# Gate matrices read back eight first keys at a time into two buffers, and scores of 88 and 80 first keys kept in DRAM

## The chip, the cores and the metric

One Trainium2 chip, one of its cores. The metric is the device time of one execution in microseconds (us), as the median of several. The core has five engines with queues of their own: PE (matrix multiplies; PEld is its weight load), DVE, ACT and POOL (element-wise work), and SP, which only issues transfers. Each engine runs its instructions in a fixed order.

## What is computed

Two layers. In each a mixer (attention, a Fourier branch and a convolution branch) is followed by an expert retrieval, and the change lies in that retrieval. There are 128 x 128 experts; an expert's number is a first key times 128 plus a second key. Every token picks 16 experts in each of 8 heads and gets for each a gate; the result sums what the chosen experts give:

```python
s_top, i_top = lax.top_k(s, PEER_TOPK)
best, pos = lax.top_k(cand, PEER_TOPK)
eid = jnp.take_along_axis(cand_id, pos, axis=-1)
gate = jax.nn.softmax(best, axis=-1).astype(hc.dtype)
u = jnp.take(u_tab, eid, axis=0)
act = jax.nn.gelu(jnp.einsum('chkd,cd->chk', u, hc)) * gate
v = jnp.take(v_tab, eid, axis=0)
return jnp.einsum('chk,chkd->cd', act, v)
```

All of it is float32: tables of 16384 x 1024 for u and for v in each layer, 512 tokens in layer 0 and 256 in layer 1.

## The kernel before, in words

Layer 0 handles its first 128 tokens by fetching the chosen rows (`gather_u`, `gather_v`: 128 fetches from u_tab and 128 from v_tab by POOL, each followed by one DVE instruction). The other 384 tokens of layer 0 and all 256 of layer 1 go the dense way: every expert's score is computed, multiplied by a gate that is zero for the experts not chosen, and multiplied with v.

Dense work runs over the 128 first keys i. For each, `scores` loads a 512 KB tile of u (L218, queue SP), splits it into a high part (`whi`, ACT, L237) and a low part (`wlo`, POOL or DVE, L243), and runs 24 matrix multiplies `su` (8 chunks, 3 each, L257 to L259). ACT applies gelu.

First stretch, `dense_u`: for the first `count` keys (`SPILL`: 92 in layer 0, 84 in layer 1) the scores go to a buffer `sst` (L978) and from there to DRAM (`sd`). Beside it, by `weave` at L1161, runs the retrieval (`retrieve`, nearly all DVE) of each group of 128 tokens and `gates`, which builds the gate matrix: 32 steps for a group, each two DVE instructions (`oij` L941, `og` L944), 8 small multiplies `pw` (L954) and one ACT copy `wst` (L957); every 8 steps a 2 MB piece goes to DRAM (`wd`). In layer 0 also 78 steps of the row fetching are woven in. `weave` writes the keys, the retrieval steps and the fetch steps in proportion: of the 92 keys of layer 0, 4 come first, 80 are spread over 246 retrieval steps, 8 follow; of the 84 of layer 1, 4, 68 over 164 steps, and 12. A scheduler then fixes each engine's order, which keeps near to the written one; `behind` keeps the fetches and the `pw` from running ahead of the keys.

Second stretch, `dense_v`: it goes over all 128 keys, first the 36 (layer 0) or 44 (layer 1) whose scores are not in DRAM, which `values` computes on the spot (`snew`, L1007), then the others, whose scores are read back (`srd`, L1010, two keys each). The gate matrices come back with `wrd` (L1026): one load brings `WB` = 4 first keys, in runs of 4 x 32 numbers, 512 bytes, 768 KB in layer 0 and 512 KB in layer 1, into one of three buffers. Per key a 512 KB tile of v is loaded and split, DVE multiplies score and gate (`xa`, L1031), ACT and DVE split the product (`xh`, `xl`), and PE adds it with 18 (layer 0) or 12 (layer 1) multiplies `yacc` into accumulators that stay over all keys. `values` runs `AHEAD` = 2 keys before its use.

Loads of u and v go through a ring of `raw` buffers, 4 KB of each partition: in `dense_u` of layer 0 four of them, in its `dense_v` two more, six (L1170, `more_rings`); in `dense_v` of layer 1 eight. A load waits on SP until the buffer's last split is done, and all that stands behind it on SP waits with it. In layer 0's `dense_u` all `wlo` are made by POOL, in layer 1's every third by DVE.

Of the kernel before, what the change touches and what calls it, by code (L numbers as in the profile page):

```python
# [9 lines left out]
F32 = mybir.dt.float32  # L10
# [15 lines left out]
P = 128  # L26
# [8 lines left out]
NCAND = 50  # L35
GRID_W = 64
TG = 32
WB = 4
OH = 4


# [107 lines left out]
def body(ctx: ExitStack, tc, nc, a, out):  # L149
# [837 lines left out]
    def dense_v(l, pp, vs, early, cols, count, sd, wd):  # L987

        c0, c1 = cols
        n = c1 - c0  # L990
        ng = n // TG

        banks = (2, 3, 4, 5, 0, 1) if l < L - 1 else range(4)
        acc = {k: (mm if at < 4 else tp)("yacc") for at, k in enumerate(banks)}
        seq = list(range(count, NK)) + list(range(count))

        def scratch():
            return pp.tile([P, n], F32, name="n0_sq", tag="xa", bufs=3)

        got = {}  # L1000

        def values(i):
            if i >= count:
                p = sm("su")
                scores(l, i, cols, p, G)
                got[i] = vs.tile([P, n], F32, name="snew", bufs=AHEAD + 1)
                S.activation(out=got[i], in_=p[:, :n], func=AF.Gelu_apprx_tanh)  # L1007
            elif i % 2 == 0:
                s = vs.tile([P, 2, n], F32, name="srd", bufs=4)
                SP.dma_start(out=s, in_=sd[i // 2])  # L1010
                got[i], got[i + 1] = s[:, 0], s[:, 1]

        def products(k, i, v, xh, xl, first, last):
            t, g = k // 2, k % 2
            mm3(acc[k], (xh[:, t * P:(t + 1) * P], xl[:, t * P:(t + 1) * P]),
                (v[0][:, g * 512:(g + 1) * 512], v[1][:, g * 512:(g + 1) * 512]), first, last)

        for i in seq[:AHEAD]:
            values(i)
        late = []  # L1020
        for at, i in enumerate(seq):
            if at + AHEAD < NK:
                values(seq[at + AHEAD])
            if i % WB == 0:
                w = vs.tile([P, ng, WB, TG], F32, name="wrd", bufs=3)
                SP.dma_start(out=w, in_=wd[:, :, i:i + WB].rearrange("g j i t -> j g i t"))  # L1026
            v = split(raw(a["v_tab"][(l * NK + i) * NK:(l * NK + i + 1) * NK]), lo_eng=V if i % 2 or l < L - 1 else G)
            x = pp.tile([P, n], F32, name="xa", bufs=3)
            xh = pp.tile([P, n], F32R, name="xh", bufs=TAIL)
            xl = pp.tile([P, n], F32R, name="xl", bufs=TAIL)  # L1030
            V.tensor_tensor(out=x.rearrange("p (g t) -> p g t", t=TG), in0=got.pop(i).rearrange("p (g t) -> p g t", t=TG), in1=w[:, :, i % WB], op=ALU.mult)  # L1031
            pace["DVE"] = split_to(xh, xl, x)
            if at < NK - TAIL:
                for k in range(len(acc)):
                    products(k, i, v, xh, xl, at == 0, False)
            else:
                late.append((i, v, xh, xl))
            yield
        early.close()
        pending = []  # L1040
        for k in banks:
            for it in late:
                products(k, *it, False, it is late[-1])
            for f in pending:
                f()
            pending = []
            if l < L - 1 and k == 0:
                order["dve"] = rsqrt(pp, rsb, pm[:, :NS], NS, 1.0 / D, "n0", [scratch()[:, :NS] for _ in range(3)])
            y = pp.tile([P, 512], F32, name="yv", bufs=2)
            S.copy(out=y, in_=acc[k])  # L1050
            f0, t0 = k % 2 * 4, c0 + k // 2 * P
            residual(l, y, f0, t0)
            if l == L - 1:
                SP.dma_start(out=out[:, f0:f0 + 4, t0 - NS:t0 - NS + P], in_=xT[:, f0:f0 + 4, t0:t0 + P])
                continue
            if k == 4:
                pm = mm("n0_cs")
            if k in (4, 5):
                for c in range(f0, f0 + 4):
                    pending.append(col_square(scratch()[:, :NS], pm[:, :NS], xT[:, c, NS:], c == 0, c == 7))  # L1060
# [27 lines left out]
            yield from g  # L1088


    SPILL = (92, 84)

    def peer(l):
        c0 = 0 if l < L - 1 else NS
# [4 lines left out]
        with pool_("gat") as gp, pool_("wp") as xp:  # L1099
            front = ExitStack()  # L1100
            qp = front.enter_context(pool_("pq"))
            qT = qp.tile([P, H, n], F32, name="pqT")
            skt = qp.tile([P, H, NK], F32, name="skt")
            SP.dma_start(out=skt, in_=a["sub_keys"][l])
            halves = [(s, s + NS) for s in range(c0, T, NS)]

            def queries(h0, h1):
                for h in range(H):
                    w = split(raw(wt[W_QRY + h]))
                    p = mm("pq")  # L1110
                    for c in range(8):
                        mm3(p[:, :NS], chunk(w, c), part(hT, c, (h0, h1)), c == 0, c == 7)
                    S.copy(out=qT[:, h, h0 - c0:h1 - c0], in_=p[:, :NS])
                    yield

            qs = queries(*halves[0])
            if len(halves) > 1:
                weave((qs, 2))
            with pool_("pn") as np_:
                if len(halves) > 1:  # L1120
                    rs = norm_stat(1, np_, halves[-1])
                    weave((qs, 2))
                    norm_mod(l, 1, np_, halves[-1], rs)
                else:
                    norm_mod(l, 1, np_, halves[-1], bc=rsb)
                    next(qs)
                    next(qs)
                    order.clear()
            drain(qs)
            more_rings(xp, *QEXTRA[l])  # L1130
            tiles = range(n // P)
            with pool_("rt") as rp:
                ciota = rp.tile([P, NCAND, TOPK], I16, name="ciota")
                SP.dma_start(out=ciota, in_=a["ciota"])
                kiota = rp.tile([P, P, 2], F16, name="kiota")
                SP.dma_start(out=kiota, in_=a["kiota"])
                res = [
                    dict(
                        eid=(gp if t * P < g else rp).tile([P, NR], F32, name="eid%d" % t),
                        gate=(gp if t * P < g else rp).tile([P, NR], F32, name="gate%d" % t),  # L1140
                    )
                    for t in tiles
                ]
                got = [retrieve(rp, qT, skt, ciota, t, r) for t, r in enumerate(res)]
                sd = dram.tile([count // 2, P, 2, n - g], F32, name="sd%d" % l)
                wd = dram.tile([(n - g) // TG, NK, NK, TG], F32, name="wd%d" % l)
                dense = [t for t in tiles if t * P >= g]
                made = [gates(rp, kiota, res[t], wd[k * P // TG:(k + 1) * P // TG]) for k, t in enumerate(dense)]
                prep = chain(got[dense[0]], *(zipped(made[k], got[t + 1] if t + 1 in tiles else iter(())) for k, t in enumerate(dense)))
                du = dense_u(l, rp, cols, count, sd)  # L1150
                pace["Pool"] = None
                if len(halves) > 1:
                    qs = queries(*halves[1])
                    weave((qs, 8), (got[0], 16))
                    drain(qs)
                weave((du, 4), (got[0], 8 if g else 0))
                fetch = iter(())
                if g:
                    drain(got[0])
                    fetch = chain(gather_u(l, gp, c0, res[0]), gather_v(l, gp, c0, res[0]))  # L1160
                weave((du, count - END[l]), (prep, PREP[l]), (fetch, FETCH[0]))  # L1161
                drain(prep)
                drain(du)
                if g:
                    more_banks()
            front.close()
            early = ExitStack()
            vs = early.enter_context(pool_("vs", side="right"))
            with pool_("vp") as vp:
                more_rings(vp, 2, VEXTRA[l])  # L1170
                dv = dense_v(l, vp, vs, early, cols, count, sd, wd)
                weave((dv, NK - count), (fetch, FETCH[1]))
                weave((dv, count), (fetch, 2 * (NR + LAG) - sum(FETCH) + FEND))
                drain(fetch)
                drain(dv)
                pace.clear()
                fewer_rings()
            fewer_rings()
# [28 lines left out]
```

## Time and profile before

| | us |
|---|---|
| median of 3 executions | 2817.54 |
| lowest, highest | 2815.96, 2826.93 |
| the profiled execution | 2819.97 |
| its span, first to last instruction | 2818.2 |
| PE busy (x16144) | 2667.3 |
| DVE busy | 2082.8 |
| POOL busy | 1336.8 |
| ACT busy | 1203.2 |
| `dense_u` of layer 0, by its first and last `su` | about 538 to 1041 |
| `dense_v` of layer 0 | about 1041 to 1715 |
| `dense_u` of layer 1 | about 2040 to 2336 |
| `dense_v` of layer 1 | about 2336 to the end |

Read it by stretch: the busy shares over the whole span (PE 95%, DVE 74%) mix stretches with different limits. Busy PE is pipelined time, so it can include slow clock and short overlaps; the idle time, which is what it leaves over, is what matters here. The rows further down give each stretch apart.

### The profile page before, as it was taken

How to read it: one execution, taken by the hardware profiler on the slowest of the kernel's cores; microseconds unless marked ns; L12 is line 12 of the kernel's file. 1: busy time of each engine (PE TensorE's matmuls, PEld its weight loads, DVE VectorE, ACT ScalarE, POOL GpSimd, SP SyncE). 2: the span in 40 equal slices, each digit the busy share in tenths (PEclk: the TensorE clock that was granted, in tenths of full speed). 3: DMA queues.
4: the chain of work that ended last, by engine and by line, in shares of the span. 5: the costliest groups of instructions: out<-in, count | busy, mean ns of one | idle time of the engine just before them, and what ended most of it. 6: DMA issues, size and time to landing. Idle time of an engine off the chain costs nothing.

```text
span 2818.2 us, 43351 instructions
## 1 busy us (share of the span) xinstructions
PE 2667.3 (95%) x16144; PEld 2320.5 (82%) x16144; DVE 2082.8 (74%) x3971; ACT 1203.2 (43%) x1940; POOL 1336.8 (47%) x725
## 2 busy tenths in 40 slices
PE   6889999977999999999999998889998999999999
PEld 3467679977899999999888886678898999998887
DVE  4665437899999738889888886876489965667665
ACT  3144534522444443333333333455454554455553
POOL 1233224555666657776322222344453547665443
PEclk8999999988999999999999999999999999999999
DMA  8622134455788879999999985335465878667884
GB/s 332 251 84 77 38 123 135 149 194 198 288 295 313 318 286 358 340 336 350 390 339 344 344 307 196 107 102 204 137 217 195 282 279 279 214 208 260 291 291 138
DMA packets 263347, 675.54 MB, mean 240 GB/s; under 512 B 20192, under 2 KB 109408, under 8 KB 260320
## 3 DMA queue, kind: packets, MB, share of 16 engines
q1 hardware_dynamic: 210720, 467.50, 48.6%
q0 software_dynamic: 36864, 134.23, 12.9%
q10 hardware_dynamic: 15552, 71.05, 6.7%
q8 instruction: 126, 2.06, 0.3%
q14 instruction: 85, 0.70, 0.1%
HBM read 600.61 MB, written 72.09 MB: 239 GB/s over the span
## 4 chain that ended last, share of the span: by engine, by line
PE 73%; DVE 20%; DMA 3%; issue 1%; ACT 1%; POOL 1%; SPq 0%; DVEq 0%; ACTq 0%; POOLq 0%
PE yacc L257 10%; PE yacc L258 10%; PE yacc L259 10%; PE su L257 7%; PE su L258 6%; PE su L259 6%; PE proj L257 3%; PE proj L258 3%; PE proj L259 3%; PE pw L954 2%; DVE rows L888 2%; DVE oh L827 1%; DVE wlo L243 1%; PE ada L324 1%; PE sc L628 1%
## 5 line engine op out<-in xcount | busy, mean ns | idle before, releaser
L243 POOL TENSOR_TENSOR wlo<-wraw,whi 128x1024 fp32r<-128x1024 f32 (+2 forms) x402 | 958.6, 2389 | 1019.9 <-ACT whi L237 986.0
L237 ACT CAST whi<-wraw 128x1024 fp32r<-128x1024 f32 (+2 forms) x676 | 677.4, 1006 | 756.2 <-PE su L258 318.5
L257 PE MATMUL su<-hT,whi 128*128 128x384 f32 (+1 forms) x2048 | 642.8, 314 | 17.9 <-ACT psc L794 14.3
L259 PE MATMUL su<-hT,wlo 128*128 128x384 f32 (+1 forms) x2048 | 637.6, 312 | 10.3 <-DVE wlo L243 9.3
L258 PE MATMUL su<-hT,whi 128*128 128x384 f32 (+1 forms) x2048 | 639.0, 312 | 0.0
L258 PE MATMUL yacc<-wlo,xh 128*128 128x512 f32 x1280 | 499.0, 390 | 0.0
L257 PE MATMUL yacc<-whi,xh 128*128 128x512 f32 x1280 | 497.4, 390 | 1.4 <-ACT xh L251 1.4
L259 PE MATMUL yacc<-whi,xl 128*128 128x512 f32 x1280 | 495.7, 390 | 0.0
L243 DVE TENSOR_TENSOR wlo<-wraw,whi 128x1024 fp32r<-128x1024 f32 (+2 forms) x274 | 347.0, 1267 | 184.0 <-ACT whi L237 179.1
L257 PEld LDWEIGHTS su<-hT,whi 128*128 128x128 f32 x2048 | 392.1, 191 | 23.0 <-ACT psc L794 14.8
L259 PEld LDWEIGHTS su<-hT,wlo 128*128 128x128 f32 x2048 | 391.4, 191 | 11.6 <-DVE wlo L243 9.7
L258 PEld LDWEIGHTS su<-hT,whi 128*128 128x128 f32 x2048 | 392.1, 191 | 2.9
L251 ACT CAST xh<-xa 128x384 fp32r<-128x384 f32 (+1 forms) x256 | 117.5, 460 | 492.4 <-issue 325.6
L252 DVE TENSOR_TENSOR xl<-xa,xh 128x384 fp32r<-128x384 f32 (+1 forms) x256 | 185.6, 727 | 148.2 <-ACT xh L251 148.1
L862 POOL DMA_INDIRECT rows<-in_v_tab,eidi x128 | 158.9, 1241 | 281.0 <-DVE acc L901 266.5
L259 PEld LDWEIGHTS yacc<-whi,xl 128*128 128x128 f32 x1280 | 240.3, 188 | 50.2
L257 PEld LDWEIGHTS yacc<-whi,xh 128*128 128x128 f32 x1280 | 240.4, 188 | 49.8 <-ACT xh L251 2.0
L258 PEld LDWEIGHTS yacc<-wlo,xh 128*128 128x128 f32 x1280 | 240.4, 188 | 47.7
L257 PE MATMUL proj<-hT,whi 128*128 128x512 f32 (+2 forms) x544 | 195.1, 361 | 17.7 <-ACT hT L251 14.7
L259 PE MATMUL proj<-hT,wlo 128*128 128x512 f32 (+2 forms) x544 | 187.9, 346 | 1.1 <-POOL wlo L243 1.1
L258 PE MATMUL proj<-hT,whi 128*128 128x512 f32 (+2 forms) x544 | 188.5, 347 | 0.5 <-DVE hT L252 0.5
L901 DVE SCALAR_TENSOR_TENSOR acc<-rows,act,acc 128x1024 f32<-128x1024 f32 x127 | 181.3, 1428 | 1.8 <-DMA rows<-in_v_tab,eidi 1.3
(273 smaller groups left out, 3962.4 us busy)
## 6 DMA issues: line engine op xcount, KB each, us to landing
wraw<-in_u_t SPq DMA_DIRECT2D x256, 512.0 KB, 4.4
wraw<-in_v_tab SPq DMA_DIRECT2D x256, 512.0 KB, 5.5
wraw<-in_wt SPq DMA_DIRECT2D x114, 512.0 KB, 3.9
wm<-in_w_mod SPq DMA_DIRECT2D x48, 1024.0 KB, 6.9
wd<-wst ACTq DMA_DIRECT2D x20, 2048.0 KB, 8.9
wrd<-wd SPq DMA_DIRECT2D x32, 768.0 KB, 9.3
sd<-sst ACTq DMA_DIRECT2D x46, 384.0 KB, 4.5
srd<-sd SPq DMA_DIRECT2D x46, 384.0 KB, 6.4
```

What stands on the lines that cost most here:

```text
L237: ins = S.copy(out=hi[:, :n], in_=r[:, :n])
L243: ins = lo_eng.tensor_tensor(out=lo[:, :n], in0=r[:, :n], in1=hi[:, :n].bitcast(F32), op=ALU.subtract)
L251: S.copy(out=hi, in_=src)
L252: return eng.tensor_tensor(out=lo, in0=src, in1=hi.bitcast(F32), op=ALU.subtract)
L257: PE.matmul(dst, lhsT=wh, rhs=xh, start=first, stop=False)
L258: PE.matmul(dst, lhsT=wh, rhs=xl, start=False, stop=False)
L259: return PE.matmul(dst, lhsT=wl, rhs=xh, start=False, stop=last)
L324: PE.matmul(acc[32 * g:32 * g + 32], lhsT=cond[:, c + g // 2, 6 - 2 * k:38 - 2 * k], rhs=w[:, g // 2, g % 2 * 512:(g % 2 + 1) * 512], star ...
L862: ins = G.indirect_dma_start(out=r, out_offset=None, in_=a[tab], in_offset=bass.IndirectOffsetOnAxis(ap=eid[:, k:k + 1], axis=0))
L888: return V.scalar_tensor_tensor(out=u, in0=u, scalar=1.0, in1=near if len(banks) == 1 else ht, op0=ALU.mult, op1=ALU.mult, accum_out=act[: ...
L901: return V.scalar_tensor_tensor(out=acc, in0=v, scalar=act[:, k:k + 1], in1=acc, op0=ALU.mult, op1=ALU.add)
L954: ins = PE.matmul(pw[:, t * NK:(t + 1) * NK], lhsT=oj[:, t // 2, :, t % 2], rhs=gg[:, k * OH // 2 + t // 2, :, t % 2], start=k == 0, stop= ...
```

## The change

The gate matrices are read back for 8 first keys at a time instead of 4: half as many loads of twice the size, in runs of 1024 bytes, into two buffers instead of three (in layer 0 a buffer is now 12 KB of each partition, in layer 1 8 KB; together 24 KB after 18 and 16 KB after 12). Since the first key of the second stretch must begin a load, `SPILL` becomes a multiple of 8: 88 and 80 keys' scores go through DRAM, and 40 and 48 keys' scores are computed in `dense_v`. In layer 0 `dense_v` gets one more raw buffer instead of two, so five in all; layer 1 keeps its eight.

```diff
-WB = 4
+WB = 8
...
             if i % WB == 0:
-                w = vs.tile([P, ng, WB, TG], F32, name="wrd", bufs=3)
+                w = vs.tile([P, ng, WB, TG], F32, name="wrd", bufs=2)
                 SP.dma_start(out=w, in_=wd[:, :, i:i + WB].rearrange("g j i t -> j g i t"))
...
-    SPILL = (92, 84)
+    SPILL = (88, 80)
...
-                more_rings(vp, 2, VEXTRA[l])
+                more_rings(vp, 1 + l, VEXTRA[l])
```

`PREP`, `FETCH` and `END`, the numbers of steps that `weave` spreads, stay as they are, so in the first stretch 76 and 64 keys are now spread over the same 246 and 164 retrieval steps.

## Rows read from the trace of the kernel before

**Rows 1.** Windows: start:end, length, busy PE PEld DVE ACT POOL, PEclk, DMA share, GB/s

```profile
538.00:684.00 146.00, 113.76 (x642) 109.52 (x641) 142.51 (x465) 46.62 (x65) 81.76 (x46) 0.87 0.58 196
684.00:900.00 216.00, 205.57 (x1438) 196.92 (x1439) 209.10 (x584) 93.08 (x146) 134.95 (x78) 0.98 0.77 282
900.00:1045.00 145.00, 143.70 (x1040) 139.45 (x1039) 90.59 (x139) 63.57 (x101) 90.20 (x49) 1.00 0.83 304
1045.00:1330.00 285.00, 284.73 (x1445) 259.64 (x1445) 242.91 (x256) 104.05 (x143) 216.84 (x131) 1.00 0.96 345
1330.00:1700.00 370.00, 370.00 (x1638) 306.43 (x1637) 308.64 (x370) 133.70 (x184) 97.90 (x82) 1.00 0.95 339
2040.00:2140.00 100.00, 90.33 (x760) 88.84 (x758) 87.14 (x299) 46.72 (x70) 51.23 (x21) 0.97 0.61 202
2140.00:2250.00 110.00, 109.25 (x1014) 107.76 (x1015) 106.52 (x274) 61.92 (x99) 50.75 (x21) 0.98 0.76 258
2250.00:2337.00 87.00, 85.50 (x836) 84.25 (x836) 52.40 (x72) 47.51 (x80) 40.73 (x17) 1.00 0.80 280
2337.00:2577.00 240.00, 238.10 (x1528) 217.10 (x1527) 157.39 (x110) 117.61 (x173) 157.74 (x64) 1.00 0.70 228
2337.00:2780.00 443.00, 441.10 (x2423) 385.21 (x2422) 292.31 (x305) 220.89 (x326) 249.92 (x101) 1.00 0.78 257
```

**Rows 2.** Waits of PE, 538 to 1045: us in total, times, longest

```profile
PE su L257 <- ACT psc L794: 14.3, 2, 11.2
PE pw L954 <- DVE og L944: 12.6, 9, 2.7
PE gtab L925 <- DVE ghere L914: 8.7, 1, 8.7
```

**Rows 3.** Waits of PE, 2040 to 2337

```profile
PE su L259 <- DVE wlo L243: 9.3, 2, 5.8
```

**Rows 4.** Timeline of ACT, 1030 to 1062: start, us; score copies of neighbouring keys

```profile
1034.24 0.48 ACT L978 ACTIVATE sst<-su 128x384 f32<-128x384 f32 x1
1038.40 0.48 ACT L978 ACTIVATE sst<-su 128x384 f32<-128x384 f32 x1
```

**Rows 5.** Timeline of ACT, 2325 to 2362: first and fourth score copy

```profile
2325.34 0.38 ACT L978 ACTIVATE sst<-su 128x256 f32<-128x256 f32 x1
...
2333.98 0.38 ACT L978 ACTIVATE sst<-su 128x256 f32<-128x256 f32 x1
```

**Rows 6.** Groups of ACT, xcount of score copies: 538-684, 684-900, 900-1045

```profile
L978 ACT ACTIVATE sst<-su 128x384 f32<-128x384 f32 x23 | 11.2, 486 | 0.0
L978 ACT ACTIVATE sst<-su 128x384 f32<-128x384 f32 x40 | 19.4, 485 | 0.0
L978 ACT ACTIVATE sst<-su 128x384 f32<-128x384 f32 x29 | 14.0, 484 | 0.0
```

**Rows 7.** The same for layer 1: 2040-2140, 2140-2250, 2250-2337

```profile
L978 ACT ACTIVATE sst<-su 128x256 f32<-128x256 f32 x30 | 11.2, 378 | 0.0
L978 ACT ACTIVATE sst<-su 128x256 f32<-128x256 f32 x31 | 11.5, 379 | 1.2 <-DMA sd<-sst 0.7 <-PE su L259 0.5
L978 ACT ACTIVATE sst<-su 128x256 f32<-128x256 f32 x24 | 9.1, 377 | 0.0
```

**Rows 8.** One DVE line, 538 to 684: ns min/median/max

```profile
L827 DVE TENSOR_TENSOR oh<-ciota,posi x16: 971/979/3102, 554.0 to 670.6; 128x800 int16<-128x800 int16 x16
```

**Rows 9.** Chain that ended last, around the start of layer 0's second stretch: start, us

```profile
1042.74 2.41 POOL wlo L243
...
1045.55 7.06 DMA wrd<-wd
...
1054.46 0.50 PE yacc L257
```

**Rows 10.** The chain at the start of layer 1's second stretch

```profile
2337.02 8.11 DMA wrd<-wd
```

**Rows 11.** DMA issues of the page: xcount, KB each, median us to landing

```profile
wraw<-in_v_tab SPq DMA_DIRECT2D x256, 512.0 KB, 5.5
```

## The prediction

> **What bounds the kernel now.** The page gives PE 2667.3 us of busy time in a span of 2818.2. That is a mean over unlike stretches, so the next view is the table of windows cut by stretch [rows 1], then the waits of PE alone [rows 2, 3], then the chain at the two places where the second stretch begins [rows 9, 10]. In the table the columns to compare are PE and DVE against the length.
>
> In both second stretches PE has nothing to gain: 284.73 of 285 and 370 of 370 us in layer 0, 441.10 of 443 in layer 1 [rows 1]. DMA is at 0.95 to 0.96 of its engines in layer 0 without PE ever waiting for it. So a lighter read-back can give back at most the few idle microseconds of these stretches: 0.3 and 2.
>
> The first stretch of layer 0 has three parts [rows 1]. From 538 to 684 DVE is busy for 142.5 of 146 us and PE idles for 32: DVE sets the pace, and PE's waits are for steps of the retrieval (`psc`, `ghere`) [rows 2]. From 684 to 900 both are nearly full, PE 205.6 and DVE 209.1 of 216. From 900 to 1045 PE is full and DVE has 54 us to spare. Layer 1 is alike: PE idles for 9.7 us up to 2140, mostly for DVE's `wlo` [rows 3]; then both are full up to 2250 (109.3 and 106.5 of 110); then PE alone.
>
> **What moves.** The four keys per layer are no new work for PE: their `su` leave a stretch in which DVE sets part of the pace and enter one where PE sets all of it. A key's `su` costs PE 1038.40 - 1034.24 = 4.16 us in layer 0 [rows 4] and (2333.98 - 2325.34) / 3 = 2.88 us in layer 1 [rows 5].
>
> Added to the second stretch, all of it on PE's path: 4 x 4.16 = **+16.6 us** in layer 0 and 4 x 2.88 = **+11.5 us** in layer 1. Nothing hides them there. The four keys' score buffers, their write to `sd` and their read-back fall away, all beside full PE: nothing.
>
> Taken from the first stretch of layer 0: `weave` thins the 80 spread keys by 5%, so the four go from everywhere. Of the 23, 40 and 29 keys of the three parts [rows 6], 19, 40 and 21 are spread ones (4 come before, 8 after), so they lose 1, 2 and 1.
> - Up to 684 DVE sets the end, and one key less gives PE only more idle time. What does help: DVE is held up where it meets POOL's split. One of its lines takes 0.971 us at the least and 3.102 at the most [rows 8], 2.1 us more; POOL's `wlo` takes 2.41 [rows 9]. A split less is worth 0 to 2.1 us to DVE; I take 0.7, since the median, 0.979, shows that most instructions meet none. Saved: 0.7.
> - From 684 to 900 PE loses 2 x 4.16 = 8.3 us of work. DVE needs its 209.1 us less 2 x 0.7, so the part can shrink from 1.4 (DVE's waits stay) to 8.3 (they all go). I take the middle, 4.8.
> - From 900 on, PE alone: 4.2.
>
> Sum 9.7 (bounds 5.6 and 14.6). Net for layer 0: 16.6 - 9.7 = **+6.9 us**.
>
> Layer 1: of 30, 31 and 24 keys [rows 7], 26, 31 and 12 are spread, thinned by 4 in 68, so they lose 1.5, 1.8 and 0.7. Up to 2140: a third of these splits is DVE's own, for which the row nearest by kind is POOL's 2.41, so 0 to 1.2 us, and I take 1.0 with the effect above. From 2140 to 2250: 1.8 x 2.88 = 5.2 at most, 1.0 at least; I take 3.0. After that 0.7 x 2.88 = 2.0. Sum 6.0 (3.0 to 8.4). Net: 11.5 - 6.0 = **+5.5 us**.
>
> **The first load of each second stretch.** PE's first `yacc` waits for a chain: POOL's `wlo` frees a raw buffer, SP issues the load behind it, then `wrd`, which lands after 7.06 us, then `xa`, `xh` and `yacc` at 1054.46 [rows 9]; in layer 1 `wrd` takes 8.11 us [rows 10]. PE fills that time with the scores of three keys, and has 0.3 us to spare in layer 0 and 2 us idle in layer 1 [rows 1]. The load is now twice as large and what is late goes straight to PE, unless the scheduler sets a fourth key's scores before it. The trace has no load of that shape. From 2250 to 2337 DMA moves 280 / 0.80 = 350 GB/s of its full time, with `wrd` among the loads (2337 to 2577) 228 / 0.70 = 326. A key there loads 1.05 MB of u and v and 0.131 MB of gates, so the gates go at about 0.131 / (1.18 / 326 - 1.05 / 350) = 0.131 / 0.00062, some 210 GB/s: an estimate from these two rows. The first load's own transfer is then 0.79 MB / 210 = 3.7 us in layer 0 and 2.5 in layer 1. Doubled, with the 1024-byte runs going at 210 to 350 GB/s, it lasts 0.8 to 3.8 us longer in layer 0 and 0.5 to 2.5 in layer 1. I take **+2** and **+1**, below the middle, since a fourth key's scores may fill it; bounds 0 and 7.06 + 8.11 = 15.2 (the whole of both times doubled).
>
> The Trainium skill, DMA: Bandwidth & Descriptors, Specifications, puts the smallest transfer for line rate at 512 B. By that, 512-byte runs already go at full rate and wider ones gain nothing; the doubled loads would cost 3.7 + 2.5 = 6.2 us instead of 3, and the sum 3 more. The rows disagree with it mildly (210 against 350 GB/s), and I keep 3.
>
> **The rest.** Five raw buffers instead of six in layer 0: a key of the later part lasts about 4.1 us (370 us and 1638 / 18 = 91 keys [rows 1]), so a buffer has 6 x 4.1 = 24.5 us from one load to the next, and will have 20.4; a load lands in 5.5 us at the median [rows 11] and its two splits take about 3. That leaves over 10 us: nothing, unless loads queue up behind the larger `wrd` on SP (a rival below). `wrd` itself waits on SP for the last `xa` of an earlier load; two buffers of eight let it go when key i - 9 is done, three of four did the same, so no wait is added and nothing new queues behind it. Row fetches per key fall in the first part of layer 0's second stretch (110 over 40 keys instead of 36) and rise a little later (76 over 88 instead of 92); PE waits for neither.
>
> **Sum.** 6.9 + 5.5 + 3 = +15.4 us on the profiled 2819.97 (span 2818.2 and 1.8 around it), 2835.4. The median of the runs is 2.4 us lower, so **2833 us**. Its own bounds: terms of the first stretches 16.6 - 14.6 + 11.5 - 8.4 = 5.1 to 16.6 - 5.6 + 11.5 - 3.0 = 19.5, loads 0 to 6.3: 2823 to 2843.
>
> **The rivals.**
> - *The first stretches shrink by all that leaves them.* If the waits of PE in 538 to 684 are an accident of the order and not DVE's pace, PE's 28.1 us come back in full and only the loads remain: +0 to +4, 2818 to 2822. For it: PE runs without a gap at 4.16 us per key between the long waits. Against: DVE's 142.5 of 146. Chance 0.22.
> - *The larger loads cost more*: both first loads take twice their whole time and PE gets no fourth key: 2817.5 + 12.4 + 15.2 = 2845. Or five raw buffers are too few: each of the 11 large loads of the later part holds the loads behind it on SP; at 2 us of starved PE each that is +22 and 2855. It decides from the point where a raw load lands later than about 17 us. For it: DMA at 0.95. Against: PE never waits for a raw load there today. Chance 0.20 together, mostly for the first.
> - *Faster, on the other side.* PE idles for 44.0 us in layer 0's first stretch [rows 1], two of the waits being 11.2 and 8.7 us long [rows 2]. The place is where the copies of `psc` and the table `gtab` are set in ACT's and PE's orders. With fewer keys between them the scheduler's order changes; if one of the two waits goes because PE finds a key to do in it, and the long ACT wait with it, that is -11 or -20 against +15.4. It decides when both go: about 2810, faster than before; with more, down to 2800. Against: in this part DVE is at 98%, so the gain must come from a better order on DVE too. Chance 0.08.
> - *The forecast*: 0.50.
>
> **How the numbers follow.** A measurement of this kernel tells about 0.5% from no change, 14.1 us, so slower begins at 2831.6 and faster ends at 2803.5. The forecast's own range, 2823 to 2843, lies on both sides: 0.23 same and 0.27 slower. The first rival adds 0.22 to same, the second 0.20 to slower, the third 0.06 to faster and 0.02 to same. So faster 0.06, same 0.47, slower 0.47. For 8 in 10 the range takes in most of the first rival, nearly all of the forecast and the first half of the second: 2815 to 2850.
>
> **What would show it.** In the changed kernel's windows both second stretches should be full on PE and longer by 16.6 and 11.5 us; the first should be shorter by about 10 and 6. The parts up to the first `gtab` of each layer should last as long as before with more idle PE. The first `yacc` should follow `wrd` directly, with a load of about 9 us. A wait of `whi` for `wraw` in layer 0's second stretch would show the ring too short. The prediction is wrong if the first stretches shrink by 28 us in sum, if a fourth key's scores hide the loads wholly, or if the order of the first stretch changes so that its long waits are others.

## The result and the profile after

The changed kernel takes 2843.84 us, the median of 4 executions (2840.31 to 2848.88), against 2819.48 for the kernel before in the same runs: 24.4 us more, a ratio of 1.009 with a 95% interval of 1.0075 to 1.0105. Forecast were 2833 and +15.4: the direction and the range of 2815 to 2850 held, and the sum was 9 us short. The forecast's own narrower bounds ended at 2843, just below the result.

The two profiled executions differ by 28.9 us of span (2818.2 and 2847.1), the medians by 24.4. Cut at events that both have, they show where:

| us, from the timelines of PE and ACT | before | changed | difference | forecast |
|---|---|---|---|---|
| to the first `su` of layer 0 | 538.5 | 540.2 | +1.7 | 0 |
| layer 0, first stretch: first `su` to last `sst` | 504.5 | 500.4 | -4.1 | -9.7 |
| gap to the first `yacc` | 11.4 | 13.5 | +2.1 | +2 |
| layer 0, second stretch: first to last `yacc` | 664.8 | 684.1 | +19.3 | +16.6 |
| mixer of layer 1 | 314.8 | 314.2 | -0.6 | 0 |
| layer 1, first stretch | 300.4 | 298.8 | -1.6 | -6.0 |
| gap to the first `yacc` | 12.5 | 12.8 | +0.3 | +1 |
| layer 1, second stretch | 465.4 | 477.0 | +11.6 | +11.5 |

The second stretches grew by what was forecast, and a little more in layer 0. The first stretches gave back less than half of what was forecast. The windows show where; they answer to [rows 1] but are cut at the gate tables (`gtab`), the points at which PE meets the retrieval. Columns as there: length, busy of PE, PEld, DVE, ACT, POOL, then PEclk, DMA share, GB/s. First the kernel before (layer 0: four parts of the first stretch, then the second stretch; layer 1: three parts and the second stretch):

```profile
538.50:677.70 139.20, 111.65 (x626) 107.84 (x624) 135.78 (x447) 45.53 (x62) 81.26 (x46) 0.89 0.60 205
677.70:812.70 135.00, 123.58 (x853) 118.30 (x853) 130.92 (x356) 54.24 (x85) 78.53 (x45) 0.95 0.72 263
812.70:939.30 126.60, 122.90 (x871) 117.84 (x871) 121.38 (x300) 55.93 (x87) 85.27 (x50) 1.00 0.83 301
939.30:1043.00 103.70, 102.40 (x757) 99.41 (x757) 53.62 (x84) 45.96 (x74) 59.34 (x33) 1.00 0.80 296
...
1054.50:1719.20 664.70, 664.70 (x3124) 572.91 (x3128) 551.93 (x640) 238.53 (x329) 307.17 (x208) 1.00 0.94 336
2034.00:2147.90 113.90, 103.57 (x855) 102.07 (x853) 94.72 (x326) 51.38 (x77) 58.74 (x24) 0.96 0.60 197
2147.90:2252.40 104.50, 102.94 (x977) 101.25 (x975) 102.73 (x249) 59.97 (x96) 51.47 (x21) 1.00 0.79 269
2252.40:2334.40 82.00, 81.97 (x807) 80.92 (x808) 50.02 (x71) 47.06 (x78) 36.34 (x16) 1.00 0.79 280
2346.80:2812.20 465.40, 465.37 (x2506) 404.31 (x2507) 301.51 (x325) 227.19 (x336) 251.52 (x102) 1.00 0.72 239
```

Then the changed kernel, with the gap to layer 0's first `yacc` as its fifth line:

```profile
540.20:681.90 141.70, 108.60 (x602) 104.78 (x600) 138.84 (x456) 44.07 (x60) 77.76 (x45) 0.87 0.58 198
681.90:810.70 128.80, 121.08 (x829) 114.72 (x829) 125.70 (x322) 53.45 (x83) 76.04 (x44) 0.96 0.75 269
810.70:943.90 133.20, 123.84 (x860) 118.60 (x859) 129.90 (x326) 55.96 (x87) 83.95 (x50) 0.97 0.80 289
943.90:1040.70 96.80, 96.80 (x720) 91.80 (x719) 53.65 (x84) 45.45 (x71) 55.34 (x30) 1.00 0.80 297
1040.70:1054.10 13.40, 11.09 (x64) 10.77 (x63) 5.26 (x4) 5.39 (x8) 9.48 (x5) 1.00 0.87 301
1054.10:1738.20 684.10, 683.89 (x3220) 590.75 (x3220) 547.90 (x639) 244.19 (x336) 321.96 (x212) 1.00 0.90 327
2052.40:2162.20 109.80, 96.84 (x809) 94.81 (x808) 92.31 (x317) 49.05 (x73) 56.91 (x23) 0.96 0.61 197
2162.20:2273.90 111.70, 105.63 (x964) 103.93 (x964) 108.66 (x256) 58.76 (x96) 46.81 (x19) 0.95 0.69 240
2273.90:2351.20 77.30, 77.30 (x771) 76.34 (x770) 48.90 (x70) 44.67 (x76) 36.28 (x16) 1.00 0.82 290
2364.00:2841.00 477.00, 476.98 (x2602) 415.77 (x2603) 306.40 (x325) 232.94 (x344) 262.26 (x106) 1.00 0.70 237
```

Call the four parts of layer 0 A, B, C and D, and the three of layer 1 E, F and G. The two orders do not put the same retrieval steps into each part: DVE has 9 instructions more in A, 34 fewer in B and 26 more in C. So A to C are compared as a sum. They last 403.7 us, 400.8 before, with DVE busy for 394.4 us, 388.1 before. PE does the scores of 69.3 keys there instead of 71.7, counted by `su`, but its busy time has fallen by 4.6 us only, since its time at the lower clock (1.2 instead of 2.4 GHz) has risen from 44.4 to 54.5 us; its idle time, the length less the busy time, has risen from 42.7 to 50.2 us. D, in which PE is full, holds 1.6 keys less and is shorter by 7.0 us. Layer 1 is alike (its first `su` is at 2034.0 before, so E begins 6 us ahead of the window in [rows 1]): E and F together last 221.5 us, 218.5 before, with DVE full in F, and G, full on PE, has shrunk by 4.6.

The waits of PE in layer 0's first stretch (total, times, longest), which answer to [rows 2]:

```profile
PE su L257 <- ACT psc L794: 15.1, 3, 11.2
PE gtab L925 <- DVE ghere L914: 13.2, 1, 13.2
PE pw L954 <- DVE og L944: 12.8, 12, 3.5
```

and in layer 1's, which answer to [rows 3]:

```profile
PE gtab L925 <- DVE ghere L914: 9.7, 1, 9.7
PE pw L954 <- DVE og L944: 5.1, 1, 5.1
PE su L259 <- DVE wlo L243: 1.9, 1, 1.9
```

Before, layer 1's first stretch had this line below that of [rows 3]:

```profile
PE gtab L925 <- DVE ghere L914: 1.5, 1, 1.5
```

PE comes to layer 0's first gate table with a key less behind it and waits there for 13.2 us instead of 8.7. In layer 1 it comes with two keys less and waits for 9.7 instead of 1.5, while its waits for `wlo` fall from 9.3 to 1.9. Most of the time taken from PE ahead of the gate tables has become PE's waiting for DVE.

The chain at the start of layer 0's second stretch, which answers to [rows 9] (start, us, what):

```profile
1043.20 9.69 DMA wrd<-wd
...
1052.99 0.57 DVE xa L1031
...
1053.58 0.52 ACT xh L251
```

The doubled load lands after 9.69 us instead of 7.06. In layer 1 it lands after 8.60 instead of the 8.11 of [rows 10].

### The profile page after: what moved, and what is told of

It is laid out like the page before. It is cut to its first block, busy times and chain, and to the rows that moved or that the text cites. A ratio compares the mean times of both kernels' runs of the same rounds, so it can differ in the third digit from the quotient of the medians.

```text
span 2847.1 us, 43303 instructions
## 1 busy us (share of the span) xinstructions
PE 2682.0 (94%) x16144; PEld 2331.1 (82%) x16144; DVE 2087.0 (73%) x3969; ACT 1207.3 (42%) x1940; POOL 1346.7 (47%) x727
## 4 chain that ended last, share of the span: by engine, by line
PE 73%; DVE 20%; DMA 4%; ACT 1%; issue 1%; POOL 1%; SPq 0%; DVEq 0%; ACTq 0%; POOLq 0%
PE yacc L258 10%; PE yacc L259 10%; PE yacc L257 10%; PE su L257 6%; PE su L259 6%; PE su L258 6%; PE proj L257 3%; PE proj L258 3%; PE proj L259 3%; DVE rows L888 2%; DVE oh L827 2%; PE pw L954 1%; PE ada L324 1%; DVE wlo L243 1%; DVE og L944 1%; DVE oij L941 1%
## 5 line engine op out<-in xcount | busy, mean ns | idle before, releaser
L257 PE MATMUL su<-hT,whi 128*128 128x384 f32 (+1 forms) x2048 | 646.4, 316 | 19.3 <-ACT psc L794 15.1
L257 PE MATMUL proj<-hT,whi 128*128 128x512 f32 (+2 forms) x544 | 195.9, 364 | 18.1 <-ACT hT L251 12.5
```

Source lines behind the costliest of these rows:

```text
L257: PE.matmul(dst, lhsT=wh, rhs=xh, start=first, stop=False)
```

## The experiments

Theory M: the cost is that of the moved keys, whose work leaves a stretch that PE does not pace. Rival R: it is that of the new read-back, in larger loads and with fewer buffers.

**The keys alone.** The kernel before with one line changed.

```diff
-    SPILL = (92, 84)
+    SPILL = (88, 80)
```

> The kernel before with 88 and 80 keys in the first stretches (SPILL alone; loads of 4 keys, three buffers and six raw buffers stay). Theory M, the moved keys cost: PE's work for four keys per layer leaves stretches that DVE paces and enters ones that PE fills. The changed kernel's traces differ by +31 us in the two second stretches and by -4 and -2 us in the first ones up to the last score copy, so this kernel should be +20 to +25 us against before. Rival R, the read-back costs (larger first loads, five raw buffers): +0 to +5 us, and the rest comes with the loads.

Measured: 2841.8 us against 2819.72, ratio 1.0072 (1.0059 to 1.0085), +22.1. The first stretches are 1.6 us shorter each, the second ones 16.9 and 11.7 longer, the gaps as before. That is what M expected: 22 of the 24 us need no edit of the read-back.

**The read-back alone.** The changed kernel with the keys put back; its first load then brings the 4 keys left of a group.

```diff
-            if i % WB == 0:
+            if i % WB == 0 or at == 0:
...
-                SP.dma_start(out=w, in_=wd[:, :, i:i + WB].rearrange("g j i t -> j g i t"))
+                SP.dma_start(out=w[:, :, i % WB:], in_=wd[:, :, i:i + WB - i % WB].rearrange("g j i t -> j g i t"))
...
-    SPILL = (88, 80)
+    SPILL = (92, 84)
```

> The changed kernel with 92 and 84 keys again, and a first load of only the 4 keys that are left of its group of 8; all other loads are of 8 keys, two buffers, five raw buffers in layer 0. Theory M: within 3 us of before, since PE fills the second stretch with or without it. Rival R: +15 to +24 us if the five raw buffers or the large loads starve PE.

Measured: 2824.57 us, ratio 1.0015 (1.0006 to 1.0024), +4.9: more than M's 3, far from R's 15. The second stretches are 663.9 and 465.4 us (before 664.8 and 465.4), the gaps 11.4 and 12.5 as before. So five raw buffers and loads of eight keys cost PE nothing there, and R falls for all but the first load, which has 4 keys here. What is longer in its profile, an execution 4.8 us above this kernel's median, lies outside the edit: 2.9 us before layer 0's first stretch, 3.9 in that stretch, whose order on PE, DVE, ACT and POOL is the same, and 3.9 in layer 1's mixer, which takes 313.0 to 320.7 us over the profiles of the kernels with fetches. What makes the 4.9 stays open.

**Four keys more in the first stretch.** The opposite step.

```diff
-    SPILL = (92, 84)
+    SPILL = (96, 88)
```

> The kernel before with 96 and 88 keys in the first stretches: four keys more there, the opposite way. Theory M: the second stretches lose 16.6 and 11.5 us; the first ones, in which DVE sets part of the pace, grow by less, some 8 to 14 and 4 to 8 us: -6 to -16 us against before. Rival O, that before just has a good order of instructions and any shift of the keys spoils it: 0 to +15 us.

Measured: 2838.47 us, ratio 1.006 (1.0047 to 1.0074), +18.8, where -6 to -16 was expected. The second stretches lost 19.7 and 11.6 us, but the first ones grew by 26.1 and 18.6, more than the four keys' own 16.6 and 11.5. Its windows, cut at the gate tables as above:

```profile
539.50:676.90 137.40, 114.66 (x642) 111.04 (x640) 134.68 (x442) 46.95 (x64) 83.75 (x47) 0.90 0.61 206
676.90:818.00 141.10, 131.06 (x885) 125.08 (x886) 135.88 (x368) 55.63 (x87) 80.44 (x46) 0.94 0.74 264
818.00:957.50 139.50, 131.84 (x902) 127.14 (x902) 123.35 (x292) 57.12 (x89) 87.70 (x51) 0.96 0.79 283
957.50:1070.20 112.70, 108.37 (x774) 103.96 (x774) 53.03 (x84) 48.70 (x76) 61.52 (x34) 0.97 0.75 273
```

PE's idle time is 44.8 us in all, after 44 before. A key more did fill part of it ahead of the first gate table (27.6 us of idle time in A before, 22.7 now), but more came back in C and D (5.0 before, 12.0 now). PE's busy time rose by 25 us, of which 16.6 are the keys; the granted clock, 1.00 in C and D before, is 0.96 and 0.97 here, and time at its lower level went from 44.4 to 61.4 us of the stretch. So M's expectation that added keys are partly free is wrong: with this order they found no idle time to fill on the whole. The rival O, that 92 and 84 keys are a good balance for this order, fits better, though +18.8 lies above its 0 to +15 too: fewer keys are not paid back, more keys are paid in full and beyond.

**Fewer fetches in the first stretch**, on the changed kernel and on the kernel before:

```diff
-    FETCH = (78, 110)
+    FETCH = (66, 122)
```

> The changed kernel with 66 instead of 78 fetch steps in the first stretch of layer 0, and 122 instead of 110 in the first part of its second (3.05 per key there, as before): 12 DVE instructions of about 1.2 us, 14.5 us in all, leave the stretch. Theory M says that DVE paces it: 5 to 12 us less than the changed kernel, that is +12 to +20 against before. Rival P, that PE's own order paces the first stretch: no change from the changed kernel, +24.

```diff
-    FETCH = (78, 110)
+    FETCH = (66, 110)
```

> The kernel before with 66 fetch steps in layer 0's first stretch instead of 78; the 12 go to the later part of the second (88 over 92 keys instead of 76), where DVE has over 60 us idle. If DVE paces the first stretch, 14.5 us of its work gone make it 5 to 10 us shorter: -4 to -10 us against before. If not, 0; and if DMA, at 0.95 there, cannot take the fetches, PE waits and it is slower.

Measured: 2841.77 us (ratio 1.0077, 1.0064 to 1.009), which cannot be told from the changed kernel's 2843.84; and 2821.39 (1.0005, 0.9996 to 1.0014), no change. In whole time both came out as expected if DVE does not pace the stretch. In the profiles the first stretch did become shorter, from 500.4 to 492.8 us in the one and from 504.5 to 501.6 in the other. In the second the rest took it back (layer 1's mixer is 5.9 us longer). In the first the span is 8.1 us shorter as well, but the profiled execution of the changed kernel was the slowest of its four, 5.0 us above the median. A to C of the first:

```profile
538.40:932.60 394.20, 349.76 (x2273) 335.73 (x2273) 379.58 (x1081) 151.72 (x228) 227.20 (x127) 0.94 0.68 241
```

DVE has 14.8 us less to do (379.6 after 394.4) and the parts last 9.5 us less (394.2 after 403.7), with PE's keys unchanged. That supports DVE's pace in the stretch, but the whole time does not show it: inconclusive as a test, and no better kernel.

**The first load cut in two**, on the changed kernel:

```diff
+                cut = (0, 4, WB) if at == 0 else (0, WB)
+                for k0, k1 in zip(cut, cut[1:]):
+                    SP.dma_start(out=w[:, :, k0:k1], in_=wd[:, :, i + k0:i + k1].rearrange("g j i t -> j g i t"))
-                SP.dma_start(out=w, in_=wd[:, :, i:i + WB].rearrange("g j i t -> j g i t"))
```

> The changed kernel with the first load of each second stretch cut into two of 4 keys each. If the size of that load costs PE time, the gap from the last score copy to the first yacc goes from 13.5 us back to about 11.5 in layer 0 and from 12.8 to about 12.5 in layer 1: 2 to 4 us less than the changed kernel, which one look cannot tell in the whole time but the gap can. If only the number of loads in flight matters, the gap stays at 13.5.

Measured: 2843.29 us in a single execution. Layer 0's gap is 11.4 us as expected, layer 1's 12.9 (no change). But layer 0's second stretch is 3.3 us longer, 687.4. From its chain and its waits of PE:

```profile
1037.53 6.15 DMA wrd<-wd
...
1050.02 14.91 DMA wraw<-in_v_tab
```

```profile
PE yacc L257 <- ACT whi L237: 2.9, 1, 2.9
```

The half-size load lands in 6.15 us, but a load of v issued soon after takes 14.91, and PE waits for that one instead. So the size of the first load does set the gap in layer 0, and in this one execution the wait moved on when it was cut; nothing is won. That the large load ahead makes the load of v late is not shown: in the kernel before two loads of v soon after that point (issued at 1064.0 and 1065.3) took 13.0 and 12.9 us too.

**Without POOL's splits in the first stretches.** The rival to plain DVE work as the pace is collision with POOL: DVE's instructions there took some 45 us longer, summed over A to C before, than the same lines and shapes take when nothing disturbs them (the tenth percentile of each). The line of [rows 8] shows one of them; so the splits were left out, at 92 and 84 and at 88 and 80 keys (the edit in part):

```diff
...
+        if first and lo_eng is G:
+            hi = ring("hi", F32R)
+            S.copy(out=hi, in_=r)
+            few = first.tile([P, 8], F32, name="few", bufs=2)
+            pace["Pool"] = G.tensor_tensor(out=few, in0=r[:, :8], in1=hi[:, :8].bitcast(F32), op=ALU.subtract)
+            w = (hi, hi)
...
```

> The kernel before without POOL's splits in the two first stretches: the low part is left out there, the three multiplies of a chunk all take the high part (the scores that go to DRAM are therefore less exact), and POOL subtracts only 8 columns, so that the order of its fetches is kept. PE's work is the same. Up to the third gate table of layer 0 DVE has 387 us of work in 401 us, and 45 us of that is what its instructions take beyond their usual time, beside POOL's splits. Theory C, these collisions set the pace of the first stretches: DVE's excess falls below 10 us, layer 0's first stretch from 504 us to 455 to 475, layer 1's from 300 to 285 to 295: -35 to -65 us against before. Rival D, the collisions fall into time that DVE has to spare: -15 to 0 us.

> The same with 88 and 80 keys in the first stretches. With the split it cost 22 us to move the keys. Theory C: without collisions PE paces most of the first stretches, so four keys less shorten them by most of 16.6 and 11.5 us, and this kernel is 0 to 10 us slower than the one with 92 and 84 keys. Rival D: 15 to 25 us slower, as with the splits.

Measured: 2799.42 us (0.9937, 0.9919 to 0.9954), -20.5, between the two ranges expected, and 2824.94 (1.0019, 1.001 to 1.0029): the keys cost 25.5 us here, just above the 15 to 25 of D. DVE's busy time in A to C fell from 388.1 to 349.6 us. The collisions are gone, which [rows 8]'s line shows in the first of the two (least, median, most):

```profile
L827 DVE TENSOR_TENSOR oh<-ciota,posi x16: 970/985/993, 548.3 to 658.5; 128x800 int16<-128x800 int16 x16
```

In layer 1, which has no fetches, the first stretch fell from 300.4 to 284.6 us, and four keys less now shorten it by 6.0 instead of 1.6, of the 11.5 that theory C would give back at most: there it holds in part. In layer 0 the stretch fell only from 504.5 to 499.6, and four keys less make it 2.2 longer. A did fall, from 139.2 to 126.4 us, but B and C grew from 261.6 to 271.7, since another wait took the collisions' place there; the wait of DVE in B and C before:

```profile
DVE rows L888 <- DMA rows<-in_u_tab,eidi: 3.8, 5, 1.6
```

and without the splits:

```profile
DVE rows L888 <- DMA rows<-in_u_tab,eidi: 38.6, 9, 9.2
```

POOL issues a fetch only behind the keys written ahead of it: each of the nine late rows was fetched right behind POOL's small subtraction of a key, which had waited for ACT's `whi` first. So a fetched row now comes too late for the faster DVE. Collisions alone are therefore not layer 0's pace, though they were part of A's, and rival D was right on the difference between 92 and 88 keys.

**Without the fetches, and without both.** The next suspect is the chain of fetches itself: it was left out, again at both numbers of keys, and then with the splits left out as well.

```diff
-                    fetch = chain(gather_u(l, gp, c0, res[0]), gather_v(l, gp, c0, res[0]))
+                    fewer_banks()
```

> The kernel before without the row fetches of layer 0: the 128 tokens of `gather_u` and `gather_v` get nothing from the experts; their retrieval and all dense work stay. DVE loses 78 instructions of 1.2 us in the first stretch, and nothing there waits for a fetched row any more. PE's work for 92 keys and 96 steps of the gate matrix is about 92 x 4.16 + 96 x 0.47 + 12 = 440 us. Theory F, retrieval and fetches together pace layer 0's first stretch: it goes from 504 us to 450 to 475, the second stays at 665: -30 to -55 us. If DVE's retrieval alone, or PE's order, sets it: less than -15.

> The same with 88 and 80 keys. Theory F: with the fetches gone PE paces layer 0's first stretch, so it gives back most of the 16.6 us that the second one gains; layer 1 still loses 10: +8 to +15 us against the kernel with 92 and 84 keys and no fetches. If any shift of the keys costs the same because the order of the instructions is spoilt, +20 to +26 as with the fetches.

> The kernel before with neither the row fetches of layer 0 nor POOL's splits in the first stretches (as in the two pairs before; the low part is left out there). PE's work is the same. Layer 0's first stretch 445 to 465 us, layer 1's about 285 as without the splits: -55 to -80 us against before.

> The same with 88 and 80 keys. If the cost of moving the keys is that DVE's work and what waits on it paces the first stretches, little of it is left here: 0 to +8 us against the kernel with 92 and 84 keys and neither. If the cost lies in the second stretches or in the order, +15 us or more.

Measured: 2776.35 us (0.9854, 0.9837 to 0.9871) and 2794.96 (0.9914, 0.9897 to 0.993) without fetches; 2753.76 (0.9767, 0.9751 to 0.9783) and 2760.63 (0.979, 0.9773 to 0.9806) without both. With 92 keys that is -43.2 and -65.8, and layer 0's first stretch lasts 472.9 and 461.1 us, all within the ranges expected: PE's own order, with the same work, does not set its 504.5. The difference that four keys make:

| us, 88 and 80 keys less 92 and 84 | as before | no splits | no fetches | neither |
|---|---|---|---|---|
| whole time, medians | +22.1 | +25.5 | +18.6 | +6.9 |
| layer 0, first stretch | -1.6 | +2.2 | -11.1 | -17.8 |
| layer 0, second stretch | +16.9 | +18.4 | +16.9 | +16.9 |
| layer 1, first stretch | -1.6 | -6.0 | -0.8 | -6.7 |
| layer 1, second stretch | +11.7 | +12.7 | +11.6 | +12.6 |

The second stretches grow by nearly the same in all four pairs (within 1.5 us). What varies is the first stretch, and in layer 0 it gives back the keys' full 16.6 us once retrieval and fetches no longer pace it. The windows with neither, A, B to D and the second stretch, at 92 and then at 88 keys:

```profile
535.50:643.30 107.80, 95.77 (x555) 94.29 (x553) 100.98 (x411) 39.95 (x55) 5.18 (x21) 0.94 0.42 142
643.30:996.60 353.30, 353.04 (x2537) 342.12 (x2537) 222.74 (x617) 158.19 (x252) 16.69 (x71) 1.00 0.60 216
1008.40:1672.20 663.80, 663.80 (x3117) 572.05 (x3120) 295.55 (x397) 239.79 (x328) 77.95 (x33) 1.00 0.61 194
```

```profile
539.60:642.30 102.70, 90.66 (x531) 89.18 (x530) 97.44 (x398) 38.51 (x53) 5.05 (x20) 0.95 0.42 141
642.30:982.90 340.60, 340.34 (x2465) 329.64 (x2465) 224.77 (x630) 153.69 (x246) 18.98 (x68) 1.00 0.61 218
994.70:1675.40 680.70, 680.70 (x3214) 588.79 (x3216) 294.67 (x397) 245.11 (x336) 86.93 (x37) 1.00 0.60 190
```

From the first gate table on PE is full in both, and 353.3 us become 340.6. That is what the first rival of the prediction forecast, for layer 0 and in a kernel without what paces this one. In layer 1 the keys give back 6.7 of 12.6 us: with four keys less PE waits once more for the first gate table, 4.0 us, and not at all with 84. Leaving out the fetches takes away both the waits for their rows and DVE's 1.2 us for each; which of the two paced layer 0 is not parted. Without fetches alone the total was expected 8 to 15 us apart, 20 to 26 by the rival, and came out between them, at 18.6: layer 0's net is +5.8, layer 1's +10.8, and 2.0 of the rest lies elsewhere.

## Why the prediction came out as it did

**What bounds the kernel; the second stretches.** Right. PE is full there in every run, to within 3.6 us of idle time, and four keys cost 16.9 and 11.7 us by themselves (forecast 16.6 and 11.5). Nothing came back from lighter DMA, whose share in layer 0 went from 0.94 over the stretch to 0.90.

**The first stretch of layer 0.** The forecast of 9.7 (bounds 5.6 and 14.6) was too high a saving. Three executions share the changed kernel's order there (it, the keys alone, the cut load): 500.4, 502.9 and 497.2 us. Two share that of before (it, the read-back alone): 504.5 and 508.4. The means differ by 6.3 us, at the low end of the bounds. By parts: A to C last 403.7, 406.2 and 400.5 against 400.8 and 406.2, 403.5 us on both sides, so what was to save 0.7 + 4.8 = 5.5 saved nothing. D saved 6.3 instead of 4.2, since 1.6 keys left it and not 1. The step that failed is the middle taken for 684 to 900: where two engines are both full and meet at fixed points, the shorter one's saving was here not half but none, as the other's chain had not become shorter. DVE's had not: the 0.7 us that each missing split was to save it did not come, with 394.4, 396.3 and 387.1 us busy in A to C against 388.1 and 391.8. Taking fetches and splits away shows it: only then do the keys pay in full.

**The first stretch of layer 1.** Forecast 6.0 (3.0 to 8.4), measured 1.2 to 1.8 in all three executions: below the bound. The term that failed is F, where DVE and PE are both full: 3.0 saved was forecast, and E and F together grew by 1 to 3 us. The idea that fewer splits free DVE had the wrong sign. DVE was busy in E and F for 197.4 us in the two executions of the order before and for 201.0 to 201.2 in the three of the changed one, with two of POOL's splits and one of its own less; without POOL's splits it is 172.9 and 171.9. So the new order met more collisions: what counts is which instructions meet a split. Without the splits four keys give back 6.0, which happens to be the forecast.

**The first loads.** Forecast +2 and +1 for the gaps, measured +2.1 and +0.3. But layer 0's second stretch is also 2.4 us longer than with the keys alone (684.1 and 681.7); the chain there has a load of v of 14.11 us right after, and PE runs 3.4 us at 1.2 GHz, where there was none before. In sum about 4.8 instead of 3. The landing, forecast at about 9 us, was 9.69. No fourth key's scores filled the gap. In layer 1's second stretch the packets of 512 bytes took 29 ns on the mean before, 279 GB/s over 16 engines; those of 1024 took 53 ns in the changed kernel, 309 GB/s; those of 4096 went at 347 and 341. Wider runs were faster there; my 210 GB/s for 512 bytes was too low. By these rates the doubled first loads last 2.3 and 1.5 us longer, an estimate; they landed 2.6 and 0.5 us later. The rule of the Trainium skill weighed there, DMA: Bandwidth & Descriptors, Specifications, that 512 B is enough for line rate, is not borne out by these packets (279 GB/s against 347).

**The rest.** Five raw buffers, two buffers of eight, fewer and larger loads: right at nothing for PE.

**The rivals.** The first (the first stretches give all back) was false here and comes true in layer 0 alone, without fetches and splits. The second, at 2845 for the first loads, comes near the result in its number but not in its mechanism: of its 15 us the loads made 5, and no raw load starved PE for long. The range held the result by its upper end, 2850, which was taken from this rival: that part was luck. By the forecast's own terms +24.4 lies just inside the upper bound, 19.5 + 6.3 = 25.8, since the first stretch of layer 0 gave back little more than its least and that of layer 1 less. The third did not happen: in layer 0 the long waits of PE stayed at the same meeting points, one of them longer. In layer 1 the long waits are others than before (`gtab` and `og` instead of `wlo`), which the prediction had named as a sign of being wrong; it is the place where the forecast lies outside its bounds.

## What to carry to other kernels

Moving work of the fullest engine out of a stretch pays only if that engine ends the stretch. Look at the meeting points (here the gate tables) and ask which engine comes there last: if it is another, the stretch keeps its length and the work costs in full where it goes. Where two engines are both full, count the saving of one as zero until a run shows otherwise. And where a number loses in both directions, as 92 keys here, look for what else holds the meeting points: without the fetches and the splits, four keys less cost 6.9 us instead of 22.1. Whether four keys more would then pay was not run.

## What had not been expected of the hardware

A small DVE instruction can wait for nearly a whole POOL split: in the kernel before, `rtab` (L807, 40 elements for each partition) took 0.18 us undisturbed and 2.35 at the most; that one started 0.1 us after a split of 2.4 and ended 0.06 us behind it. Once POOL subtracted 8 columns only, no instruction of that line took longer than 0.29 us in layer 0's first stretch.

And in the changed kernel PE's idle times of 3.37, 13.22, 3.49, 3.17 and 3.42 us in layer 0's first stretch each had a time at 1.2 GHz begin in them or within 0.5 us behind them, so such a wait costs again where PE has to catch up. Four keys more than before raised PE's busy time by 25 us, 8 more than their work, with 17 us more at 1.2 GHz.
